# A decoder layer with a mixture of experts: four experts in the last unit, its last product in halves, the last norm's rows spread by the tensor engine

## The chip, the cores and the metric

The kernel runs on one core of one Trainium2 chip. The metric is the device time of one execution in microseconds (us). Before the change the median of three runs is 1271.21 us (1270.5 to 1271.6).

Engines as the profile names them: PE is the tensor engine's matmul side (TensorE), PEld its weight loads, DVE the vector engine, ACT the scalar engine, POOL GpSimd, SP the engine that issues most DMAs. A "q" behind a name (SPq) is that engine's sequencer.

## The reference

One layer of a decoder: a token-mixing part (two kinds of attention, an output projection and a norm) and then a mixture of experts with a last norm. The change touches only the end of the second part:

```python
h = _layer_norm(x) * (1 + sc2[:, None]) + sh2[:, None]
y = (1 + g2[:, None]) * _hier_moe(h, ...)          # 32 experts, two for each of 512 tokens
x = _layer_norm(ALPHA * x + y) * ln2_g[l] + ln2_b[l]

def expert_block(args):                            # in _hier_moe
    xb, e = args
    return (jax.nn.silu(xb @ w1[e]) * (xb @ w3[e])) @ w2[e]
```

The data is float32: 512 tokens of 1024 features, each expert has w1 and w3 of 1024 x 512 and w2 of 512 x 1024, 2 MB each, 6 MB an expert.

## The kernel before

All 32 experts' weights are read, some 200 MB. The experts are sorted by how many tokens they got, and worked in **units** of 128 token slots: one expert with 128 slots, two with 64 or four with 32. After two fixed units (-2 and -1) the list `ORDER` says in which order the eleven others come. A unit number of 2 to 6 is a pair (64 slots each), 7 to 10 a unit of four (32 slots each); before, the list ends with unit 10 (four experts) and unit 6 (two).

**Loads.** `load_unit` (L1249) issues a unit's weights on SP's queue: t counts 0 to 11, four tiles of 512 KB for each of w1, w3 and w2 and each expert, so 24 tiles for a pair and 48 for four. Tiles come from a ring of 36 buffers (`Q`, which other tiles share), in order of allocation. A plain tile is `src[:, j * 1024:(j + 1) * 1024]`, a contiguous 4 KB for each of 128 partitions. With `quarters` (the last unit) a tile of w2 holds 256 of the 1024 output columns for all four row blocks k, which is four pieces of 1 KB for each partition: 512 pieces a tile (L1266). Every 512 KB tile is one DMA.

**Work of a unit.** `up` makes silu(x w1) * (x w3) on PE, ACT and DVE; between the two products (`mid=between`) the previous unit's results are added to the four accumulators `acc[i]` (128 tokens x 1024) by `combine`. `down_lhs` transposes the result (`pat` to `aT`) and the routing weights (`ptw` to `pT`). For four experts each product runs on 32 columns of the array (form 128*32), for two on 64 (128*64).

**The last unit** has its own product with w2, in four quarters q of 256 columns. `quarter_up` makes `py` (8 products), `weighted_halves` (L1493 to L1496) makes `y` (DVE), its rounded copy `yh` (ACT) and the rest `yl` (DVE); `quarter_add` spreads them over the tokens by eight products `pcb` (yh and yl for four token tiles) and adds them to `acc`, with a running sum for the norm (L1665). `squares` (ACT, L1647) makes the sums of squares around a shift `nsh`, which is a mean from quarter 0. Each engine works strictly in the order of the code. With q equal to 3, between `y` and the adds, stands `overflow()`: a loop over leftover blocks with a count read at run time, where all engines meet (L1542); in this data it has no turn.

**The last norm.** `l2g` and `l2b`, its weight and bias, are read by `row_bc` (L1632, L1633): a DMA on POOL's queue that reads one row of 4 KB 128 times, once for each partition, 512 KB each. `bh` and `bl` are row 0 of `l2b`, rounded and rest. Behind the adds come small DVE operations on `l3`, `less_mean` (L1702) for four token tiles, Ln and Exp on ACT for the deviation, and then two token tiles finish on PE and ACT (`pcl`, L1721) and two on DVE (L1726), each half with a store.

## Time and profile before

| | us |
|---|---|
| runs: median (lowest to highest) | 1271.21 (1270.5 to 1271.6) |
| the profiled execution's own time | 1270.36 |
| its span, first to last instruction | 1268.6 |
| last 512 KB tile in 4 KB pieces issued | 1214.74 |
| first and last quarter tile issued | 1216.67 and 1229.66 |
| first and last quarter's `py` begins | 1230.59 and 1244.25 |
| last `yl` (before the loop) begins | 1248.84 |
| last add of the last unit begins | 1252.44 |

The profile is one execution. Its first page gives busy shares in 40 slices of the span, 31.7 us each; the timeline lists instructions by start, with duration, and in brackets how long the engine was idle before and what ended it. A `x16` behind a float32 product counts profiler records, two for a product in the code. The windows view gives each engine's busy time in a stretch, then the granted TensorE clock (1.00 is 2.4 GHz, 0.50 is 1.2 GHz), the busy share of the DMA engines and the bytes they moved.

### The profile page before, as it was taken

The page shows a single profiled execution, that of the slowest core. Times are in us where ns is not written, and L with a number is a line of the kernel's source. Part 1 is how long each engine was busy: PE and PEld are TensorE (multiplying, and loading weights), DVE is VectorE, ACT ScalarE, POOL GpSimd, SP SyncE. Part 2 cuts the span into 40 slices and gives each one's busy share as a digit, 9 for nine tenths or more (in the row PEclk, how much of TensorE's full clock was granted, in tenths as well). Part 3 has the DMA queues.
Part 4 walks back from the last instruction along what each step waited for, and adds up shares of the span by engine and source line. Part 5 has one row for each costly group of instructions (what it writes and reads, how often), then busy time and mean ns, then how long its engine had stood idle before and what let it go on. Part 6 is the DMA issues. An engine that isn't in the chain of part 4 may idle for free. (4 is left out here: it accounts for less than half of the span.)

```text
span 1268.6 us, 18601 instructions
## 1 busy us (share of the span) xinstructions
PE 1182.0 (93%) x6663; PEld 817.7 (64%) x6663; DVE 698.9 (55%) x1624; ACT 426.1 (34%) x907; POOL 117.2 (9%) x175
## 2 busy tenths in 40 slices
PE   5999999999999999999989969999999899999885
PEld 4788898778888888878768963434335235354233
DVE  5564988887565665323586787435135144444045
ACT  4333666664435264554131421201102002021004
POOL 3011111111101011001150140000000000000000
PEclk8999999999999999999998979999999999999998
DMA  9954313324334253335324098999999999999991
GB/s 323 297 148 145 114 58 117 104 88 129 108 113 120 68 167 100 100 120 184 116 84 183 26 356 304 409 408 409 409 409 409 409 409 408 405 406 409 401 329 68
DMA packets 140863, 297.14 MB, mean 234 GB/s; under 512 B 11100, under 2 KB 82980, under 8 KB 140769
## 3 DMA queue, kind: packets, MB, share of 16 engines
q1 hardware_dynamic: 131296, 268.57, 57.6%
q0 software_dynamic: 8704, 25.00, 6.1%
q10 hardware_dynamic: 768, 2.37, 0.5%
q8 instruction: 53, 0.87, 0.3%
q14 instruction: 42, 0.34, 0.1%
HBM read 293.76 MB, written 4.76 MB: 235 GB/s over the span
## 5 line engine op out<-in xcount | busy, mean ns | idle before, releaser
L183 PE MATMUL p<-ew,xe 128*32 128x512 f32 (+1 forms) x960 | 196.7, 597 | 12.5 <-DMA ew<-in_exp_w_dram 12.4
L276 DVE TENSOR_TENSOR wl<-wst,wh 128x1024 fp32r<-128x1024 f32 (+1 forms) x93 | 126.1, 1385 | 74.7 <-ACT wh L275 73.8
L183 PEld LDWEIGHTS p<-ew,xe 128*32 128x32 f32 (+1 forms) x960 | 53.6, 122 | 149.0 <-issue 79.3
L183 PE MATMUL py<-ew,aT 128*32 128x512 f32 (+2 forms) x496 | 101.6, 571 | 9.3 <-DMA ew<-in_exp_w_dram 6.5
L1472 DVE TENSOR_TENSOR s<-s,p 128x512 f32<-128x512 f32 x13 | 8.9, 688 | 173.2 <-PE p L183 157.4
L275 ACT ACTIVATE wh<-wst 128x1024 fp32r<-128x1024 f32 (+1 forms) x94 | 93.0, 1030 | 28.9 <-POOL wst L274 16.6
L183 PEld LDWEIGHTS py<-ew,aT 128*32 128x32 f32 (+1 forms) x496 | 27.3, 122 | 76.3 <-DMA ew<-in_exp_w_dram 35.9
L1521 DVE TENSOR_TENSOR acc<-acc,pcb 128x512 f32<-128x512 f32 x96 | 58.3, 681 | 15.2 <-PE pcb L181 15.2
L1480 ACT ACTIVATE aT<-pat 128x512 f32<-128x512 f32 x13 | 7.8, 597 | 171.9 <-PE pat L187 171.9
L1495 ACT ACTIVATE yh<-y 128x512 fp32r<-128x512 f32 (+1 forms) x28 | 16.8, 599 | 141.9 <-DVE y L1493 131.8
L181 PE MATMUL pgx<-pm,xhh 128*128 128x256 f32 (+1 forms) x224 | 56.3, 293 | 2.1 <-DVE pm L1241 2.1
L1493 DVE SCALAR_TENSOR_TENSOR y<-py,cs,g2b 128x512 f32<-128x512 f32 (+1 forms) x28 | 19.9, 710 | 65.6 <-PE py L183 65.4
L181 PE MATMUL pgx<-pm,xhl 128*128 128x256 f32 (+1 forms) x224 | 54.6, 286 | 0.0
L514 POOL DMA_DIRECT2D adaw<-in_ada_w_dram x64 | 34.6, 542 | 196.6 <-PE ptp L187 44.0
L181 PE MATMUL pcb<-yh,pT 128*128 128x512 f32 (+1 forms) x112 | 44.6, 400 | 6.9 <-DVEq L1542 3.6
L181 PE MATMUL pmg<-hh,wh 128*128 128x512 f32 x128 | 50.4, 394 | 0.0
L181 PE MATMUL psg<-hh,wh 128*128 128x512 f32 x128 | 50.3, 393 | 0.0
L181 PE MATMUL psg<-hl,wh 128*128 128x512 f32 x128 | 49.9, 390 | 0.0
L181 PE MATMUL psg<-hh,wl 128*128 128x512 f32 x128 | 49.9, 390 | 0.0
L181 PE MATMUL pmg<-hh,wl 128*128 128x512 f32 x128 | 49.9, 390 | 0.0
L181 PE MATMUL pmg<-hl,wh 128*128 128x512 f32 x128 | 49.8, 389 | 0.0
L181 PEld LDWEIGHTS pgx<-pm,xhh 128*128 128x128 f32 x224 | 43.8, 196 | 5.6 <-DVE pm L1241 2.5
(520 smaller groups left out, 2872.8 us busy)
## 6 DMA issues: line engine op xcount, KB each, us to landing
ew<-in_exp_w_dram SPq DMA_DIRECT2D x380, 512.0 KB, 10.1
wst<-in_w_in_dram SPq DMA_DIRECT2D x66, 512.0 KB, 4.7
adaw<-in_ada_w_dram POOLq DMA_DIRECT2D x64, 256.0 KB, 3.1
adaw<-in_ada_w_dram SPq DMA_DIRECT2D x16, 512.0 KB, 9.2
wst<-in_w_br_hg_dram SPq DMA_DIRECT2D x8, 512.0 KB, 4.0
wst<-in_w_br_nsa_dram SPq DMA_DIRECT2D x8, 512.0 KB, 4.1
wst<-in_w_out_dram SPq DMA_DIRECT2D x8, 512.0 KB, 4.9
ext_d<-ext_d POOLq DMA_DIRECT2D x1, 2560.0 KB, 17.1
```

Of the source, the lines that this page charges most:

```text
L181: PE.matmul(o, l, r, start=start, stop=stop)
L183: PE.matmul(o, l, r, start=start, stop=stop, tile_position=pos)
L275: A.activation(wh, self.w[j], AF.Copy)
L276: (sub or V).tensor_sub(wl, self.w[j], wh.bitcast(F32))
L514: P_.dma_start(w, ada[:, k, 2048 + j * 512:2560 + j * 512])
L1472: V.tensor_mul(s1, s1, p3)
L1480: A.activation(aT, at_.rearrange("p (f s) -> p f s", f=4), AF.Copy)
L1493: V.scalar_tensor_tensor(y, py, cs_, g2b[c0 // 512][:, c0 % 512:c0 % 512 + n], op0=OP.mult, op1=OP.mult)
L1495: A.activation(yh, y, AF.Copy)
L1521: V.tensor_add(acc[i][:, s_], acc[i][:, s_], pc_)
```

## The change

`ORDER` swaps its last two units, so the pair 6 comes before the unit of four 10, and the last unit loads 48 tiles where it loaded 24. Its w2 is loaded in halves: a tile holds 512 columns for two row blocks, two pieces of 2 KB for each partition, 256 pieces a tile. The tiles come in the order first half (8 tiles: two row-block pairs times four experts), second half (8 tiles).

The last product runs in two pieces of 512 columns, `half_up` and `half_add`, where there were four of 256. The first half's sums give `nsh`, and its squares come before the second half; the loop stands before the second half's adds. `l2g` and `l2b` are loaded as single rows (`l2r`, 4 KB on one partition each). While the second half's weights come in, ACT and DVE split both rows into a rounded part and a rest (`l2h`, `l2l`), PE multiplies them by a row of ones (eight products into four `pl2` tiles), and ACT copies these into `l2g` and `l2b`. The final steps are as before, with one small addition less.

```diff
-ORDER = [7, 0, 8, 1, 9, 2, 3, 4, 5, 10, 6]
+ORDER = [7, 0, 8, 1, 9, 2, 3, 4, 5, 6, 10]
...
-                if quarters and t >= 8:
-                    nc.sync.dma_start(w.rearrange("p (k n) -> p k n", k=4),
-                                      src.rearrange("p (k n) -> p k n", k=4)[:, :, j * 256:(j + 1) * 256])
+                if halves and t >= 8:
+                    kk, c0 = j % 2 * 2, j // 2 * 512
+                    nc.sync.dma_start(w.rearrange("p (k n) -> p k n", k=2),
+                                      src.rearrange("p (k n) -> p k n", k=4)[:, kk:kk + 2, c0:c0 + 512])
...
-    l2g = row_bc("l2g", a["ln2_g"])
-    l2b = row_bc("l2b", a["ln2_b"])
+    l2r = [Q(n_)[0:1, :] for n_ in ("l2gr", "l2br")]
+    for t, name in zip(l2r, ("ln2_g", "ln2_b")):
+        P_.dma_start(t, a[name])
...
+    def half_up(h):
+        py = PS("py")
         m = 128 // len(w_now["exp_w2"])
         for k in range(4):
             for x, w in enumerate(w_now["exp_w2"]):
-                mm(py[m * x:m * x + m, :], aT[:, k, m * x:m * x + m], w[q][:, k * 256:(k + 1) * 256], k == 0, k == 3,
-                   pos=(0, m * x) if m < 128 else None)
+                mm(py[m * x:m * x + m, :], aT[:, k, m * x:m * x + m], w[2 * h + k // 2][:, k % 2 * 512:k % 2 * 512 + 512],
+                   k == 0, k == 3, pos=(0, m * x) if m < 128 else None)
...
-    for q in range(4):
-        py = quarter_up(q)
-        y = quarter_y(q, py)
-        if q == 3:
-            overflow()
-            A.preload_act_table_set("natural_log_exp_and_others")
-            V.tensor_reduce(l3[:, :, 4:5], sums[:, :, 0:3], axis=AX.X, op=OP.add)
-        if q == 2:
-            for i in range(NT):
-                squares(i, 0)
-        if q == 1:
-            oner, bh, bl = (Q(n_, F32R)[0:1, :] for n_ in ("oner", "l2h", "l2l"))
-            A.activation(oner[:, 0:128], ones[0:1, :], AF.Copy)
-            A.activation(bh, l2b[0:1, :], AF.Copy)
-            V.tensor_sub(bl, l2b[0:1, :], bh.bitcast(F32))
-        for i in range(NT):
-            quarter_add(q, y, i)
-            if q > 1:
-                squares(i, q - 1)
-        if q == 0:
-            V.tensor_scalar(nsh, sums[:, :, 0], -1.0 / 256, None, op0=OP.mult)
+    py = half_up(0)
+    y = weighted_halves(py, cs_, 0, 512)
+    oner = Q("oner", F32R)[0:1, 0:128]
+    A.activation(oner, ones[0:1, :], AF.Copy)
+    l2h, l2l = ([Q(n_, F32R)[0:1, :] for n_ in ns] for ns in (("l2gh", "l2bh"), ("l2gl", "l2bl")))
+    for t, h_, l_ in zip(l2r, l2h, l2l):
+        A.activation(h_, t, AF.Copy)
+        V.tensor_sub(l_, t, h_.bitcast(F32))
+    for i in range(NT):
+        half_add(0, y, i)
+    V.tensor_scalar(nsh, sums[:, :, 0], -1.0 / 512, None, op0=OP.mult)
+    l2g, l2b = Q("l2g"), Q("l2b")
+    for t, h_, l_ in zip((l2g, l2b), l2h, l2l):
+        for s_ in halves_:
+            ps = PS("pl2")
+            for j, x in enumerate((h_, l_)):
+                mm(ps, oner, x[:, s_], j == 0, j == 1)
+            A.activation(t[:, s_], ps, AF.Copy)
+    for i in range(NT):
+        squares(i, 0)
+    py = half_up(1)
+    y = weighted_halves(py, cs_, 512, 512)
+    overflow()
+    A.preload_act_table_set("natural_log_exp_and_others")
+    for i in range(NT):
+        half_add(1, y, i)
+        squares(i, 1)
...
-    V.tensor_add(l3[:, :, 3], sqs[:, :, 0], sqs[:, :, 1])
```

Where the instructions go, at two places. First ScalarE (ACT), from the rounded copy `yh` of quarter 1 (with the change: of the first half) to the last `yh` before the loop. Here `sq` are the squares, `acc_6756` and its likes the four token tiles, and the column counts at the end tell quarters (256) from halves (512). Before:

```order
L1495 ACTIVATE yh_10857<-y_10855 128x256
L1684 ACTIVATE oner_10861<-ones_94 1x128
L1685 ACTIVATE l2h_10862<-l2b_10791 1x1024
L1495 ACTIVATE yh_10894<-y_10892 128x256
L1647 ACTIVATE sq_10812,sqs_10811<-acc_6756,nsh_10813 128x512
...
L1647 ACTIVATE sq_10812,sqs_10811<-acc_7244,nsh_10813 128x512
L1647 ACTIVATE sq_10812,sqs_10811<-acc_6756,nsh_10813 128x256
...
L1647 ACTIVATE sq_10812,sqs_10811<-acc_7244,nsh_10813 128x256
L1495 ACTIVATE yh_10933<-y_10931 128x256
```

The same stretch with the change:

```order
L1496 ACTIVATE yh_10817<-y_10815 128x512
L1673 ACTIVATE oner_10821<-ones_94 1x128
L1676 ACTIVATE l2gh_10823<-l2gr_10773 1x1024
L1676 ACTIVATE l2bh_10824<-l2br_10774 1x1024
L1687 ACTIVATE l2g_10848<-pl2_10850 128x512
...
L1687 ACTIVATE l2b_10849<-pl2_10862 128x512
L1648 ACTIVATE sq_10796,sqs_10795<-acc_6756,nsh_10797 128x512
...
L1648 ACTIVATE sq_10796,sqs_10795<-acc_7244,nsh_10797 128x512
L1496 ACTIVATE yh_10889<-y_10887 128x512
```

The eight squares that stood ahead of the last `yh` are four, and ahead of them stand the split of a second row and four copies out of `pl2`.

Second PE, from the product before the last one to the loop, where `py` is the product with w2 (`ew` the weights), `pcb` the spread over the tokens. Before:

```order
L183 MATMUL py<-ew,aT 64x256 x8
L181 MATMUL pcb<-yh,pT 128x256
L181 MATMUL pcb<-yl,pT 128x256
...
L183 MATMUL py<-ew,aT 64x256 x8
L1542 COMPARE_AND_BRANCH
```

With the change (the `pl_` tiles are the `pl2` of the code):

```order
L183 MATMUL py<-ew,aT 32x512 x16
L181 MATMUL pcb<-yh,pT 128x512
L181 MATMUL pcb<-yl,pT 128x512
...
L181 MATMUL pl_10850<-l2gh,oner 128x512
L181 MATMUL pl_10850<-l2gl,oner 128x512
...
L181 MATMUL pl_10862<-l2bh,oner 128x512
L181 MATMUL pl_10862<-l2bl,oner 128x512
L183 MATMUL py<-ew,aT 32x512 x16
L1543 COMPARE_AND_BRANCH
```

Eight products `pl2` now stand between the first half's `pcb` and the second half's `py`, and each `py` is sixteen products of 512 columns in place of eight of 256.

## Rows read from the trace of the kernel before

**Rows 1.** Page, part 2: busy tenths of the DMA engines in 40 slices.

```profile
DMA  9954313324334253335324098999999999999991
```

**Rows 2.** Windows: busy us (instructions), PE PEld DVE ACT POOL; clock; DMA share, GB/s.

```profile
30.00:40.00 10.00, 10.00 (x72) 7.71 (x70) 2.75 (x6) 1.52 (x2) 0.00 (x0) 1.00 1.09 348
1200.00:1205.00 5.00, 4.54 (x16) 0.82 (x16) 0.75 (x1) 0.54 (x1) 0.00 (x0) 1.00 1.02 405
1240.00:1245.00 5.00, 3.69 (x32) 2.33 (x28) 3.98 (x18) 2.64 (x7) 0.00 (x0) 1.00 0.00 0
1245.00:1250.00 5.00, 1.42 (x13) 0.75 (x10) 1.02 (x5) 3.64 (x13) 0.00 (x0) 0.94 0.02 5
1250.00:1256.00 6.00, 5.56 (x16) 4.00 (x16) 4.41 (x18) 4.28 (x12) 0.00 (x0) 0.50 0.00 1
```

**Rows 3.** SP's issues of L1269, 1191 to 1206 us and 1190 to 1215 us.

```profile
L1269 SPq DMA_DIRECT2D ew<-in_exp_w_dram x13: 333/333/337, 1191.1 to 1206.4; - x13
...
DMA to landing us min/median/max: 9.6/10.1/12.7
...
L1269 SPq DMA_DIRECT2D ew<-in_exp_w_dram x19: 332/333/337, 1189.9 to 1214.7; - x19
```

**Rows 4.** Timeline of POOL, 1206 us: the first of two row loads.

```profile
1206.60 0.59 POOL L973 DMA_DIRECT2D l2g<-in_ln_g_dram  x1 [448.68 <-DVE y L1493]
```

**Rows 5.** SP's issues of L1266, quarter tiles: ns min/median/max, times.

```profile
L1266 SPq DMA_DIRECT2D ew<-in_exp_w_dram x8: 543/1180/3129, 1216.7 to 1229.7; - x8
```

**Rows 6.** Timeline of the last unit (start, us, engine, line): first and last quarter.

```profile
1230.59 1.95 PE L183 MATMUL py<-ew,aT 128*64 128x256 f32 x16 [0.25 <-ACT aT L1480]
...
1244.25 1.95 PE L183 MATMUL py<-ew,aT 128*64 128x256 f32 x16
...
1248.40 0.40 ACT L1495 ACTIVATE yh<-y 128x256 fp32r<-128x256 f32 x1
1248.84 0.43 DVE L1496 TENSOR_TENSOR yl<-y,yh 128x256 fp32r<-128x256 f32 x1 [2.10 <-ACTq L1542]
```

**Rows 7.** Timeline behind the loop: adds, row products, the norm's last products.

```profile
1249.78 0.58 PE L181 MATMUL pcb<-yh,pT 128*128 128x256 f32 x1 [3.58 <-DVEq L1542]
...
1251.34 0.17 DVE L1677 TENSOR_REDUCE l<-sums 128x4 f32<-128x12 f32 x1 [2.07 <-PE pcb L181]
...
1252.38 0.62 PE L181 MATMUL pcl<-l2l,oner 1*128 1x512 f32 x1
...
1252.44 0.42 DVE L1665 CUSTOM_DVE_ANT_0 acc<-acc,pcb 128x256 f32<-128x256 f32 x1
...
1252.80 0.62 PE L181 MATMUL pcl<-l2h,oner 1*128 1x512 f32 x1
...
1256.37 5.30 PE L181 MATMUL pcl<-acc,dg 128*128 128x512 f32 x8 [0.81 <-ACT dg L1715]
```

**Rows 8.** Timeline of earlier units: y, yh, yl, eight adds, py of 512 columns.

```profile
937.83 0.75 DVE L1493 SCALAR_TENSOR_TENSOR y<-py,cs,g2b 128x512 f32<-128x512 f32 x1 [13.31 <-PE py L183]
...
938.62 0.63 ACT L1495 ACTIVATE yh<-y 128x512 fp32r<-128x512 f32 x1 [14.82 <-DVE y L1493]
...
939.28 0.69 DVE L1496 TENSOR_TENSOR yl<-y,yh 128x512 fp32r<-128x512 f32 x1 [0.69 <-ACT yh L1495]
...
953.29 4.86 DVE L1521 TENSOR_TENSOR acc<-acc,pcb 128x512 f32<-128x512 f32 x8
...
1202.53 1.90 PE L183 MATMUL py<-ew,aT 128*32 128x512 f32 x10 [0.24 <-DMA ew<-in_exp_w_dram]
```

**Rows 9.** Timeline of the last unit: the split of a row, the squares.

```profile
1238.15 1.04 ACT L1685 ACTIVATE l2h<-l2b 1x1024 fp32r<-1x1024 f32 x1
...
1239.23 1.21 DVE L1686 TENSOR_TENSOR l2l<-l2b,l2h 1x1024 fp32r<-1x1024 f32 x1 [0.72 <-ACT l2h L1685]
...
1242.62 0.71 ACT L1647 ACTIVATE sq<-acc,nsh 128x512 f32<-128x512 f32 x1
...
1246.00 0.51 ACT L1647 ACTIVATE sq<-acc,nsh 128x256 f32<-128x256 f32 x1
```

More of the change, by code (lines that the diff above doesn't have):

```diff
@@ L1247, in expert_rows, with load_unit @@
         return a[name][0][ds(e, 1)].rearrange("e (p k) n -> p (e k n)", p=128)
-    def load_unit(es, lo=0, hi=12, res=None, quarters=False):
+    def load_unit(es, lo=0, hi=12, res=None, halves=False):
         res = res or {n: [[] for _ in es] for n in ("exp_w1", "exp_w3", "exp_w2")}
@@ L1561, in overflow @@
             for i in range(NT):
-                V.tensor_reduce(sums[:, i, 0:3], acc[i][:, 0:768].rearrange("p (q n) -> p q n", q=3), axis=AX.X, op=OP.add)
+                V.tensor_reduce(sums[:, i, 0:1], acc[i][:, 0:512], axis=AX.X, op=OP.add)
                 squares(i, 0)
-                squares(i, 1)
         S = s_ring
@@ L1615, in hybrid_kernel @@
             es = tuple(ev(4 * v_ - 16 + x) for x in range(4))
-        w_now, quarters = ws, n + 2 == len(units)
-        ws = load_unit(es, quarters=quarters)
+        w_now, halves = ws, n + 2 == len(units)
+        ws = load_unit(es, halves=halves)
         if n > 1:
@@ L1630, in hybrid_kernel, with squares @@
     w_now = ws
-    l2g = row_bc("l2g", a["ln2_g"])
-    l2b = row_bc("l2b", a["ln2_b"])
+    l2r = [Q(n_)[0:1, :] for n_ in ("l2gr", "l2br")]
+    for t, name in zip(l2r, ("ln2_g", "ln2_b")):
+        P_.dma_start(t, a[name])
     aT, pT, cs_ = down_lhs(act, pw)
     l3 = cp.tile([128, NT, 6], F32, name="l3")
-    sums = cp.tile([128, NT, 4], F32, name="sums")
-    sqs = cp.tile([128, NT, 3], F32, name="sqs")
+    sums = cp.tile([128, NT, 2], F32, name="sums")
+    sqs = cp.tile([128, NT, 2], F32, name="sqs")
     sq = S("sq")
     nsh = cp.tile([128, NT], F32, name="nsh")
-    def squares(i, j):
-        c0, n = ((0, 512), (512, 256), (768, 256))[j]
-        A.activation(sq[:, 0:n], acc[i][:, c0:c0 + n], AF.Square, bias=nsh[:, i:i + 1], accum_out=sqs[:, i, j:j + 1])
-    def quarter_up(q):
-        py = PS("py")[:, 0:256]
+    halves_ = [slice(0, 512), slice(512, 1024)]
+    def squares(i, h):
+        A.activation(sq, acc[i][:, halves_[h]], AF.Square, bias=nsh[:, i:i + 1], accum_out=sqs[:, i, h:h + 1])
+    def half_up(h):
+        py = PS("py")
         m = 128 // len(w_now["exp_w2"])
@@ L1654, in quarter_up @@
             for x, w in enumerate(w_now["exp_w2"]):
-                mm(py[m * x:m * x + m, :], aT[:, k, m * x:m * x + m], w[q][:, k * 256:(k + 1) * 256], k == 0, k == 3,
-                   pos=(0, m * x) if m < 128 else None)
-        return py
-    def quarter_add(q, y, i):
-        pc_ = PS("pcb")[:, 0:256]
+                mm(py[m * x:m * x + m, :], aT[:, k, m * x:m * x + m], w[2 * h + k // 2][:, k % 2 * 512:k % 2 * 512 + 512],
+                   k == 0, k == 3, pos=(0, m * x) if m < 128 else None)
@@ L1662, in quarter_add, with half_add @@
+        return py
+    def half_add(h, y, i):
+        pc_ = PS("pcb")
         for j, t in enumerate(y):
             mm(pc_, pT[:, i * 128:(i + 1) * 128], t, j == 0, j == 1)
-        z = acc[i][:, q * 256:(q + 1) * 256]
+        z = acc[i][:, halves_[h]]
         V.tensor_tensor_reduce(out=z, in0=z, in1=pc_, scale=1.0, scalar=0.0, op0=OP.add, op1=OP.add,
-                               accum_out=sums[:, i, q:q + 1])
-    def quarter_y(q, py):
-        return weighted_halves(py, cs_, q * 256, 256)
@@ L1694, in hybrid_kernel @@
-    V.tensor_add(l3[:, :, 0], sums[:, :, 3], l3[:, :, 4])
+                               accum_out=sums[:, i, h:h + 1])
+    py = half_up(0)
[8 more added lines that the diff above has]
+        half_add(0, y, i)
@@ L1695, in hybrid_kernel @@
+    for i in range(NT):
+        half_add(1, y, i)
+        squares(i, 1)
+    V.tensor_add(l3[:, :, 0], sums[:, :, 0], sums[:, :, 1])
     V.scalar_tensor_tensor(l3[:, :, 2], l3[:, :, 0], 1.0 / D, nsh, op0=OP.mult, op1=OP.add)
     V.tensor_mul(l3[:, :, 2], l3[:, :, 2], l3[:, :, 2])
-    V.tensor_add(l3[:, :, 3], sqs[:, :, 0], sqs[:, :, 1])
-    V.scalar_tensor_tensor(l3[:, :, 5], l3[:, :, 3], 1.0 / D, l3[:, :, 2], op0=OP.mult, op1=OP.subtract)
+    V.scalar_tensor_tensor(l3[:, :, 5], sqs[:, :, 0], 1.0 / D, l3[:, :, 2], op0=OP.mult, op1=OP.subtract)
@@ L1703, in hybrid_kernel @@
     less_mean(0)
-    V.scalar_tensor_tensor(l3[:, :, 1], sqs[:, :, 2], 1.0 / D, l3[:, :, 5], op0=OP.mult, op1=OP.add)
+    V.scalar_tensor_tensor(l3[:, :, 1], sqs[:, :, 1], 1.0 / D, l3[:, :, 5], op0=OP.mult, op1=OP.add)
     A.activation(l3[:, :, 2], l3[:, :, 1], AF.Ln, bias=eps[:, 0:1])
@@ L1708, in hybrid_kernel @@
     dg = S("dg")[:, 0:256].rearrange("p (i t) -> p i t", i=2)
-    halves_ = [slice(0, 512), slice(512, 1024)]
     pcl = {(i, h): PS("pcl") for i in range(2) for h in range(2)}
     for (i, h), ps in pcl.items():
-        for j, b_ in enumerate((bh, bl)):
+        for j, b_ in enumerate((l2h[1], l2l[1])):
             mm(ps, oner[:, 0:128], b_[:, halves_[h]], j == 0, False)
```

## The prediction

> **What bounds the kernel now.** I read the page's slices first. From slice 24 on (about 760 us) the DMA engines stand at nine tenths or more almost to the end, and only the last slice is empty [rows 1]: in this stretch the experts' weights set the pace. The windows say how fast: 405 GB/s between 1200 and 1205 us, nothing at all from 1240 us [rows 2]. So the kernel ends in two parts, a stream that ends before 1240 us and some 30 us of work behind it, and the question is what in that work waits for weights.
>
> SP's issues give the stream's pace: 13 tiles of 512 KB from 1191.1 to 1206.4 us, which is 12 steps of 1.275 us, each landing 10.1 us after its issue [rows 3]. The nineteen issues up to 1214.7 us take 24.8 us where 18 such steps are 23.0 [rows 3]; between them POOL issued the two spread row loads [rows 4].
>
> Then the last unit. Its first quarter starts at 1230.59 us, its fourth at 1244.25 [rows 6]: 4.55 us a quarter, with 1.95 us of PE in it. The last quarter tile was issued at 1229.7 us [rows 5], and the fourth quarter starts over 4 us after the last bytes have moved [rows 2]. The quarters wait for each other, not for weights: py, y, yh, yl, spread, next py, each on another engine. The last `yh` moreover starts at 1248.40 us without an idle time of ACT ahead of it [rows 6], so it stood in line behind the eight squares. `yl` ends at 1248.84 + 0.43 = 1249.27 us; call this point **E**. From E to the end of the span it is 19.3 us: the loop, the adds (the last ends at 1252.44 + 0.42 = 1252.86 us [rows 7]) and the norm with its stores.
>
> **The change, step by step.** With a unit of four last, 16 tiles of w2 come behind the last tile of w3. The first half's product, its spread and the rows then have time while the second half loads, so E should follow the end of the stream. Call the landing of the last tile T.
>
> *The stream's end.* The 1206.4 us issue was ahead of the spread row loads; it lands at 1206.4 + 10.1 = 1216.5 us. Five of the 19 issues in rows 3 come after it (19 less 13 and the one at 1189.9), and the eight quarter tiles [rows 5], so 13 tiles follow. The change swaps two units, not the number of tiles. The two spread loads, 1 MB, are gone from the 16 engines, two steps or 2.55 us; two rows of 4 KB are nothing. The tiles of w2 are now in 2 KB pieces, which this trace doesn't show in a full stream. Bounds: 4 KB pieces at 1.275 us a tile [rows 3]; 1 KB pieces (the 256-column loads of the start) at 348 GB/s between 30 and 40 us [rows 2], 524,288 B / 348 = 1.507 us. A tile has 128, 256 or 512 pieces, so I go by a price for each piece: 1.275 + 0.232 x 128/384 = 1.352 us. The two tiles ahead of the 13 are halves too, 0.15 us more. T = 1216.5 + 13 x 1.352 + 0.15 = **1234.2** us (bounds 1233.1 and 1236.6).
>
> The Trainium skill (DMA: Bandwidth & Descriptors, Specifications) gives 512 B as the smallest transfer at line rate; by that rule halves would cost as much as whole rows, and quarters too. The trace speaks against it for 1 KB.
>
> *From T to E.* The order of the products is row block, then expert, so behind the last tile five products are left. In earlier units of four the same five (ten records) took 1.90 us from the landing [rows 8]. Then y, yh, yl of 512 columns: from 937.83 to 939.28 + 0.69, 2.14 us [rows 8], and 0.05 us to start. E = 1234.2 + 1.90 + 0.05 + 2.14 = **1238.3** us, against 1249.27: **11.0 us earlier**.
>
> *What has to be hidden before.* The first half's last tile lands at T - 8 x 1.352 = 1223.4 us; aT is ready long before, since w3 ended eight tiles earlier still. py ends at 1225.3, the first yh at 1226.8 (0.84 to its start, 0.63 [rows 8]). On ACT follow two row splits of 1.04, on DVE two rests of 1.21 [rows 9]: DVE is through at about 1230.5, because the adds stand behind the rests in DVE's order. Four adds of 512 at 4.86/8 = 0.61 us [rows 8] and nsh: 1233.2. The spread's eight products on PE and four copies on ACT (0.6 each, as yh) fit before that. Then four squares, 1246.00 - 1242.62 = 3.38 us with their reads [rows 9]: ACT is free at 1236.6, and the second yh wants it at 1234.2 + 1.90 + 0.05 + 0.79 = 1236.9. Cover 0.3 us: it costs nothing, but each microsecond more on this side chain costs nearly one. On PE the eleven products of the second half whose tiles have landed stand behind the spread; they begin at about 1231.5 and end about when T comes.
>
> *Behind E.* The loop stays. PE's first product starts 0.51 us after E (1249.78), DVE's first operation 2.07 us after it (1251.34) [rows 7]. Before, the adds then ended 3.59 us after E. Now they have 512 columns. The clock has fallen to half here [rows 2], where row products of 512 columns start 0.42 us apart (1252.38, 1252.80 [rows 7]); four pairs end at 0.51 + 7 x 0.425 + 0.62 = 4.1 us, and the last add, some 0.15 + 0.69 us, at 4.95. That is **1.36 us later** than before. The smaller DVE chain (one small addition) I leave at nothing; from the last add on I take the old 15.74 us.
>
> *Sum.* 1268.6 - 11.0 + 1.36 = **1259.0** us of span. The profiled execution has 1.76 us beside its span (1270.36), and the median of the runs lies 0.85 us above that execution: 1259.0 + 1.76 + 0.85 = **1261.6** us.
>
> **The rivals.**
>
> *The clock stays up.* PE idles 3.58 us ahead of the first spread product behind the loop [rows 7], and the granted clock goes from 0.94 to 0.50 in those windows [rows 2]: that is the fall from 2.4 to 1.2 GHz. With the change PE ends its last product at 1236.1 and starts again at 1238.8, 2.7 us. If that isn't idle enough, the pairs come 0.43 us apart and DVE sets the adds: 2.07 + 4 x 0.61 + 0.1 = 4.6 (-0.35), and the norm's last products, 5.30 us at mostly half clock [rows 7], lose up to 1.9, of which DVE's two token tiles, that end nearly as late, let through about 1.2. Time 1261.6 - 1.5 = **1260.1**. For it: the gap is shorter. Against: PE has little to do in the gap's neighbourhood either. The Trainium skill (TensorE: Matmul & The Clock Gate, part 1) says that throttled is the default state and activity releases it, which leaves both open.
>
> *Halves at full rate.* If a piece of 2 KB costs no more than its bytes, the 16 tiles come at the 1.275 us of whole rows [rows 3]: T is 1233.1, the time 1261.6 - 1.1 = **1260.5**. For it: whole rows show no price for their own pieces. Against: 1 KB pieces have one [rows 2]. This is also what the Trainium skill's rule above would make of it.
>
> *The side chain comes late.* If the row splits, adds and squares take 2.3 us longer than my sum (a late row, a PSUM buffer not free, squares that wait), the second yh waits 2 us for ACT: **1263.6**. For it: a margin of 0.3 us. Against: all durations are from rows.
>
> *The stream's end doesn't move as said*: the share of the two spread loads isn't won, because the ring of 36 buffers holds up a last unit of 48 tiles for as long. T is then 2.55 us later, the time **1264.2**. Against: units of four ran at the full pace with the same ring, as the slices before the end show [rows 1].
>
> *SP's issues stall, slower than before.* Quarter tiles cost SP 0.54 to 3.13 us to issue, 1.86 us apart in the mean (1216.7 to 1229.7 in seven steps [rows 5]) against 0.33 for a whole tile [rows 3]. With the change this falls on 16 tiles of which the last binds. At 1.86 us a tile T is 13 x 0.51 = 6.6 us later, **1268.2**. At 2.28 us a tile the change is slower by 0.2%; at 2.7, the upper half of what rows 5 show, the time is 1261.6 + 13 x 1.37 = **1279.4**. For it: halves still have twice the pieces of whole rows. Against: at the start 1 KB pieces kept 348 GB/s [rows 2].
>
> **How the numbers follow.** Forecast 1261.6: 0.45. Clock stays: 0.2. Halves at full rate: 0.1. Side chain late: 0.12. Stream's end unmoved: 0.05. Stalls: 0.08, of which 0.03 end on the slower side and 0.01 within. The runs can tell about 0.2% (2.5 us) from no change. Faster: 0.96; same 0.01; slower 0.03. The range goes from 1258.5 (4 KB rate and the clock up, with the side chain then binding) to 1266.0 (past the upper bound of T, 1261.6 + 2.4, and the unmoved stream); it leaves out the stalls and the tails of the rest, under 2 in 10.
>
> **What would show it.** Right: the last `ew` tile lands near 1234 us, `py` starts its last five products only then, the last `yl` ends about 4.1 us later, ACT has a short idle time or none ahead of the last `yh`, and the last add ends 4.6 to 5 us behind `yl`. SP's half tiles should issue about 1.35 us apart, with issues under 1 us. Wrong: issues of 2 us or more; a `yh` that follows the squares without a gap and late; a stream whose end stays at 1238 us; or an end part that isn't as long as before.

## The result, and the profile after

The changed kernel takes 1264.83 us (median of seven runs, 1261.01 to 1266.71) where the kernel before, run beside it, takes 1270.5 (1269.99 to 1271.6): a ratio of 0.995, 95% interval 0.9937 to 0.9963. The forecast was 1261.6 with a range of 1258.5 to 1266.0. The profiled execution took 1264.83 us with a span of 1263.0, 4.0 more than the 1259.0 of the sum.

First the page's slices of the kernel after, to be held against [rows 1]: the granted clock and the DMA engines' busy tenths.

```profile
PEclk9999999999999999999998989999999999999996
DMA  9954314234334243335335097999999999999991
```

The stream still fills the end up to the last slice. SP's issues of the half tiles, which answer to [rows 3] and [rows 5] (times in ns: min/median/max):

```profile
L1267 SPq DMA_DIRECT2D ew<-in_exp_w_dram x16: 372/413/1245, 1202.3 to 1222.8; - x16
...
DMA to landing us min/median/max: 10.3/11.0/11.5
```

Sixteen issues from 1202.26 to 1222.83 us are 15 steps of 1.371 us. The last tile lands 10.5 us after its issue, so T is 1233.3 us. Now the timeline, which answers to [rows 6], [rows 7] and [rows 9]:

```profile
1222.75 1.90 PE L183 MATMUL py<-ew,aT 128*32 128x512 f32 x10 [1.03 <-DMA ew<-in_exp_w_dram]
...
1226.16 0.49 PE L181 MATMUL pcb<-yh,pT 128*128 128x512 f32 x1 [1.50 <-ACT yh L1496]
...
1229.37 0.79 PE L181 MATMUL pl<-l2gh,oner 1*128 1x512 f32 x1
...
1232.53 0.62 PE L181 MATMUL pl<-l2bl,oner 1*128 1x512 f32 x1
...
1233.08 6.11 PE L183 MATMUL py<-ew,aT 128*32 128x512 f32 x32
...
1236.84 0.18 ACT L1648 ACTIVATION_READ_ACCUMULATOR sq<-acc,nsh 128x1 f32 x1
...
1240.05 0.63 ACT L1496 ACTIVATE yh<-y 128x512 fp32r<-128x512 f32 x1 [3.02 <-DVE y L1494]
1240.71 0.69 DVE L1497 TENSOR_TENSOR yl<-y,yh 128x512 fp32r<-128x512 f32 x1 [0.70 <-ACTq L1543]
...
1241.97 0.80 PE L181 MATMUL pcb<-yh,pT 128*128 128x512 f32 x1 [2.78 <-DVEq L1543]
...
1245.55 0.68 DVE L1666 CUSTOM_DVE_ANT_0 acc<-acc,pcb 128x512 f32<-128x512 f32 x1
...
1249.67 6.42 PE L181 MATMUL pcl<-acc,dg 128*128 128x512 f32 x8 [2.19 <-ACT dg L1717]
```

E is 1240.71 + 0.69 = 1241.40 us (1241.41 unrounded). The second half's sixteen products (x32) run in one piece, without any wait for a DMA, from 1233.08 to 1239.19 us. So the last tile, at 1233.3, was not what they waited for: PE came late to them, and was slow. ACT, for which the prediction had 0.3 us of cover, waited 3.02 us for their `y`. The windows of the same kernel, one microsecond each, with the columns of [rows 2], show why:

```profile
1225.00:1226.00 1.00, 0.00 (x0) 0.00 (x0) 0.44 (x1) 0.52 (x1) 0.00 (x0) 1.00 1.06 391
1226.00:1227.00 1.00, 0.61 (x2) 0.30 (x3) 0.69 (x1) 1.00 (x3) 0.00 (x0) 1.00 0.95 348
1227.00:1228.00 1.00, 1.00 (x5) 0.78 (x6) 0.71 (x1) 1.00 (x2) 0.00 (x0) 0.93 0.38 145
1228.00:1229.00 1.00, 1.00 (x4) 0.63 (x2) 1.00 (x2) 0.20 (x1) 0.00 (x0) 0.50 0.11 43
...
1232.00:1233.00 1.00, 1.00 (x3) 0.33 (x2) 0.23 (x3) 0.68 (x2) 0.00 (x0) 0.50 0.05 18
```

The clock falls to 1.2 GHz between 1227 and 1228 us and stays there until 1238.1. Ahead of it PE had run the first half's product with waits of about a third of a microsecond to one for tiles, and had idled 1.5 us for `y` and `yh`. The last two columns show something else: the bytes all but stop at 1227.5 us, and 18 to 43 GB/s trickle until the last tile is in, over 5 us later. The trace's semaphore records tell more of it. A tile has landed when its semaphore has been raised sixteen times; for the last tile fifteen of these fall between 1227.00 and 1229.00 us, and the sixteenth comes alone at 1233.28. In the eleven profiled executions with halves the last tile's sixteenth comes 3.9 to 4.8 us behind its fifteenth. That fits one of the core's 16 DMA engines that ends late (385 / 16 = 24 GB/s, about the trickle); which engine it is, and why, is not shown.

The change's 19 runs beside all the experiments (1261.01 to 1267.64, median 1264.48) fall in two groups with nothing between: eight up to 1262.79 and eleven from 1264.42. Three of the 19 executions are profiled; what is known of the cause is told with e12 and behind the experiments.

### The profile page after: what moved, and what is told of

Same layout as the page of the kernel before. It is cut to its first block, busy times and chain, and to the rows that moved or that the text cites. A ratio compares the mean times of both kernels' runs of the same rounds, so it can differ in the third digit from the quotient of the medians.

```text
span 1263.0 us, 18494 instructions
## 1 busy us (share of the span) xinstructions
PE 1178.2 (93%) x6623; PEld 815.2 (65%) x6623; DVE 696.5 (55%) x1603; ACT 428.0 (34%) x902; POOL 115.5 (9%) x175
## 5 line engine op out<-in xcount | busy, mean ns | idle before, releaser
L276 DVE TENSOR_TENSOR wl<-wst,wh 128x1024 fp32r<-128x1024 f32 (+1 forms) x93 | 119.6, 1315 | 74.8 <-ACT wh L275 74.1
L183 PE MATMUL py<-ew,aT 128*32 128x512 f32 (+1 forms) x464 | 98.1, 621 | 8.8 <-DMA ew<-in_exp_w_dram 6.0
L1496 ACT ACTIVATE yh<-y 128x512 fp32r<-128x512 f32 x26 | 16.4, 631 | 133.8 <-DVE y L1494 122.2
L1494 DVE SCALAR_TENSOR_TENSOR y<-py,cs,g2b 128x512 f32<-128x512 f32 x26 | 19.4, 748 | 66.3 <-PE py L183 66.1
L181 PE MATMUL pcb<-yh,pT 128*128 128x512 f32 x104 | 43.8, 422 | 4.3 <-DVEq L1543 2.8
```

Source lines behind the costliest of these rows:

```text
L181: PE.matmul(o, l, r, start=start, stop=stop)
L183: PE.matmul(o, l, r, start=start, stop=stop, tile_position=pos)
L276: (sub or V).tensor_sub(wl, self.w[j], wh.bitcast(F32))
L1494: V.scalar_tensor_tensor(y, py, cs_, g2b[c0 // 512][:, c0 % 512:c0 % 512 + n], op0=OP.mult, op1=OP.mult)
L1496: A.activation(yh, y, AF.Copy)
```

## The experiments

Theory: E comes late because PE's clock is at half ahead of and during the second half's product; with the clock up, that product waits for T and E is T + 4.1 as forecast. Rivals: the slow last landing sets E whatever the clock; the new order gives nothing and the gain is that of halves and rows; the order gives it all. One number tells the first two apart: E behind the last tile's issue. The measured landing of 10.5 us and the 4.1 us of the prediction make 14.6; the profile above has 18.58. "Unread products" are products of 512 columns on the whole array whose result nothing reads.

All profiled executions in one table (us). S is the issue of the first tile behind the pause that ends the routing stage, where the even stream starts: 766.60 in before.

| kernel | ratio to before (95%) | S | last issue, S + | E, S + | E behind last issue | last add, E + | from there to the end |
|---|---|---|---|---|---|---|---|
| before | 1 | 766.60 | 463.1 | 482.7 | 19.60 | 3.60 | 15.72 |
| after | 0.9950 (0.9937, 0.9963) | 765.35 | 457.5 | 476.1 | 18.58 | 4.83 | 16.73 |
| e7, after again | 0.9948 (0.9933, 0.9965) | 768.84 | 456.9 | 475.5 | 18.58 | 4.78 | 16.75 |
| e12, after again | 0.9941 (0.9926, 0.9956) | 767.96 | 456.6 | 471.2 | 14.54 | 4.63 | 16.03 |
| e2, order only | 0.9956 (0.9941, 0.9970) | 767.63 | 463.7 | 475.8 | 12.12 | 3.93 | 16.62 |
| e3, pair last | 0.9977 (0.9965, 0.9988) | 767.70 | 456.8 | 476.9 | 20.06 | 4.63 | 16.50 |
| e4, spread loads | 0.9951 (0.9936, 0.9965) | 767.12 | 459.4 | 473.9 | 14.55 | 4.63 | 15.84 |
| e1, unread products | 0.9946 (0.9929, 0.9962) | 765.34 | 456.5 | 471.0 | 14.55 | 5.73 | 14.04 |
| e8, e1 again | one run | 767.29 | 457.1 | 472.6 | 15.49 | 6.01 | 17.60 |
| e5, bias late | 0.9940 (0.9926, 0.9955) | 767.65 | 457.2 | 471.7 | 14.56 | 4.63 | 17.95 |
| e6, unread between | 0.9981 (0.9968, 0.9993) | 767.65 | 456.5 | 477.5 | 21.04 | 5.42 | 15.50 |
| e9, late and 11 unread | 0.9936 (0.9922, 0.9950) | 767.67 | 456.6 | 471.1 | 14.56 | 5.44 | 15.60 |
| e11, late and 6 unread | 0.9924 (0.9911, 0.9938) | 767.38 | 457.0 | 471.6 | 14.56 | 4.63 | 16.64 |
| e10, before and 12 unread | 1.0005 (0.9996, 1.0014) | 767.13 | 462.4 | 482.0 | 19.60 | 4.05 | 16.88 |

**e1: unread products in three places.**

```diff
     py = half_up(0)
+    warm(6)                  # 6 unread products
...
     py = half_up(1)
+    warm(10)
...
     # behind the norm's bias products pcl
+    warm(8)
```

> Edit: products whose result nobody reads are put into PE's idle times of the changed kernel: 6 behind the first half's product, 10 behind the second half's, 8 behind the bias products of the norm. In the changed kernel's trace the granted clock is at half from 1227.8 to 1238.1 us and again around the adds and the norm's last products; PE had waited for y and yh ahead of each fall. Theory A (the fallen clock makes PE the last to arrive: the second half's product takes 6.1 us and ends 5.9 us behind the landing of the last tile, 1222.8 + 10.5 = 1233.3): with the clock up the product ends 1.9 us behind that landing, so about 4 us earlier, the adds about 0.3 and the last products about 1.5 earlier: a span of about 1257.5, time near 1259, and the runs closer together. Theory B (the stream's end and the length of the chain set the time, the clock is a side effect): span 1262 to 1264, no change within 0.1%.

E came 14.55 us behind the last issue, not 18.58, at a clock that stayed up until 1252.2 us; the profiled execution took 1257.89 us, the shortest of all runs. The norm's products show what the clock is worth there:

```profile
1245.51 3.70 PE L181 MATMUL pcl<-acc,dg 128*128 128x512 f32 x8 [0.52 <-ACT dg L1725]
```

3.70 us where the kernel after took 6.42. The last tile took the same 10.4 us to land, so the rival that the landing sets E at 18.6 falls. But the median is 1263.73 and three of six runs lie above 1264.4: the unread products did not hold the clock each time, and the ten in front of the loop cost the adds 0.9 us (E + 5.73).

**e2: the new order alone**, in the kernel before.

```diff
-ORDER = [7, 0, 8, 1, 9, 2, 3, 4, 5, 10, 6]
+ORDER = [7, 0, 8, 1, 9, 2, 3, 4, 5, 6, 10]
```

> Edit: the kernel before with only the order of the last two units swapped; four quarters, quarter tiles in 1 KB pieces and the two spread row loads as before. Theory A (the order makes the stream's end the point from which the tail counts): the stream has 16 quarter tiles and 1 MB of row loads, so its last tile lands at 1239 (1.5 us a tile) to 1244 us (1.86 us a tile, as the eight quarter tiles before); E follows 3.5 us later, and the end 19.3 us after E: span 1262 to 1266.5, some 2 to 6 us faster than before. Theory C (the order is worth nothing by itself, the halves and the row loads make the gain): span 1268 to 1270.

The order alone gives a ratio of 0.9956, nearly the whole gain of the median. SP's issues of its sixteen quarter tiles, and the timeline up to the last `yl`:

```profile
L1266 SPq DMA_DIRECT2D ew<-in_exp_w_dram x16: 543/1183/5711, 1204.1 to 1231.3; - x16
```

```profile
1239.81 1.92 PE L183 MATMUL py<-ew,aT 128*32 128x256 f32 x26 [0.75 <-SPq L1542]
...
1242.07 0.51 ACT L1647 ACTIVATE sq<-acc,nsh 128x256 f32<-128x256 f32 x1
...
1242.58 0.40 ACT L1495 ACTIVATE yh<-y 128x256 fp32r<-128x256 f32 x1
1243.01 0.43 DVE L1496 TENSOR_TENSOR yl<-y,yh 128x256 fp32r<-128x256 f32 x1 [0.77 <-ACTq L1542]
```

With four quarters behind the stream, the order by itself brings E 6.9 us nearer to S. But its last issue is 6.2 us later than in the kernel after. The sixteen tiles of 1 KB pieces come 1.81 us apart (27.2 us in 15 steps), where halves take 1.37. Not all of this is the price of the pieces, because the two spread row loads, 1 MB, run in the same stretch. POOL issues the first here, and only 1 KB pieces of weights move in the windows from 1220 us on (columns as in [rows 2]):

```profile
1209.21 0.59 POOL L973 DMA_DIRECT2D l2g<-in_ln_g_dram  x1 [451.01 <-DMA ew<-in_exp_w_dram]
```

```profile
1220.00:1225.00 5.00, 3.86 (x28) 1.38 (x28) 0.25 (x1) 0.00 (x0) 0.00 (x0) 0.68 0.94 309
1225.00:1230.00 5.00, 3.42 (x40) 2.52 (x40) 2.77 (x12) 0.57 (x2) 0.00 (x0) 0.98 1.05 332
1230.00:1235.00 5.00, 3.72 (x34) 2.04 (x38) 3.00 (x10) 1.41 (x3) 0.00 (x0) 1.00 1.05 343
```

309 to 343 GB/s are 1.53 to 1.70 us a tile. `yh`, again without an idle time ahead of it, stands behind eight squares. One thing more sets this kernel apart: its times are 2.45 to 2.70 us above their spans in all six runs, those of every other kernel 1.73 to 1.91. By the span (median 1263.5, the 19 runs of the changed kernel 1262.6) the order alone is nearer still to the whole change. Where the 0.7 us come from is not shown.

**e3: everything but the order.** The changed kernel with the old `ORDER`, so halves and rows with a pair last (the e2 line the other way round).

> Edit: the changed kernel with the old order, the pair last, so with halves and single rows only. Theory A: the pair's work isn't bound by loads; w3 lands 2.5 us earlier than before (no spread row loads), and two serial halves with the split of the rows between them take about as long as four quarters less the squares: E near 1244 and a span near 1264, 1 us slower than the changed kernel and 4 to 5 us faster than before; so most of the gain is the halves and the row loads, and the order adds little. Theory D (the order is the whole gain): span 1267 or more.

The ratio is 0.9977, about half of the gain or less. The span of 1265.7 us is neither that of theory A (1264) nor that of theory D (1267 or more). Its timeline:

```profile
1238.44 3.65 PE L183 MATMUL py<-ew,aT 128*64 128x512 f32 x16
...
1242.14 0.75 DVE L1494 SCALAR_TENSOR_TENSOR y<-py,cs,g2b 128x512 f32<-128x512 f32 x1 [2.17 <-PE py L183]
...
1242.54 0.72 ACT L1648 ACTIVATE sq<-acc,nsh 128x512 f32<-128x512 f32 x1
...
1243.26 0.61 ACT L1496 ACTIVATE yh<-y 128x512 fp32r<-128x512 f32 x1
```

The whole product of the second half (3.65 us, no wait for a tile) comes behind the spread, and `yh` behind four squares: E is 20.1 us behind the last issue. With a pair, w3 ends only eight tiles before the end, so the first half's chain is not over when the last tile lands. The order alone (0.44%) and halves with rows alone (0.23%) each pay, and together they come to more than the whole change (0.50 to 0.59%), though the intervals leave room for a plain sum. That both shorten the same stretch is likely, not shown.

**e4: the two spread loads back**, no rows spread by PE, in the changed kernel.

```diff
+    l2g = row_bc("l2g", a["ln2_g"])
+    l2b = row_bc("l2b", a["ln2_b"])
-    l2r = ...                # the rows' loads, the split of the weight's row
-    ...                      # eight products pl2, four copies
```

> Edit: the changed kernel with the two rows loaded 128 times each by POOL again, and without the split of the weight row, the eight products that spread the rows and the four copies. Theory A (PE, not the stream, arrives last in the changed kernel): the stream ends 2.5 us later, at about 1235.9, but PE has 3.7 us less ahead of the second half's product; E is at 1240 to 1241.5 against 1241.4, span 1261.5 to 1263: the same as the changed kernel. Theory B (the stream's end sets the time): 2.5 us slower than the changed kernel, span near 1265.5.

The last tile is issued at S + 459.4, 1.9 to 2.9 us later than in the changed kernel's other forms: that is the price of the two loads (2.55 in the prediction). But PE's clock stayed up through the second half's product here, and E is again 14.55 us behind the last issue. E and the span (1241.06 and 1261.5 us) are where theory A had them, but not for its reason: E follows the landing by 4.1 us, so here the stream sets it. The median, 1264.72 us, is that of the changed kernel. Rows instead of spread loads won nothing in the median. That the eight products of one row and 512 columns ahead of the second half take back what the stream gives, whenever the clock is low there, fits this but is not shown by the medians.

**e5: the bias row's spread moved** behind the norm's bias products, where PE waits.

```diff
-    for t, h_, l_ in zip((l2g, l2b), l2h, l2l):   # 8 products, 4 copies
+    # 4 products and 2 copies for l2g here
...
+    pl2b = spread(1)         # 4 products for l2b, behind the products pcl
```

> Edit: in the changed kernel the bias row's four spread products and its two copies are moved from ahead of the second half's product to behind the bias products of the norm, where PE waited 2.2 us and ACT 1.9 us in the changed kernel's trace. Theory A (PE arrives last): the second half's product starts four row products earlier, 0.9 us at the full clock and 1.7 at half, and ACT is free 1.2 us earlier: span 1261 to 1262, 0.1% faster than the changed kernel. Theory B (the stream's end sets the time): no change.

E behind the last issue is 14.56 us, 4.0 less than in the kernel after, and no run is above 1264.23 us. The median is 1263.76 us, beside 1264.73 of e7 in the same set, with intervals that overlap. The clock then falls behind E (1240.7 to 1254.4 us at 1.2 GHz), the norm's products take 6.59 us, and the end comes 17.95 us after the last add: 1.2 of the 4.0 are given back there.

**e6: e5 with unread products between the products of the first half**, and with six behind that half, ten behind the second and four behind the late bias products.

```diff
             mm(py[m * x:m * x + m, :], ...)
+            if fill and k % 2 == 0 and k + x < 5:
+                warm(fill)   # 3 unread products behind each of 7 products
```

> Edit: the kernel e5_bias_late with unread products in PE's waits: three behind each of the first products of the first half that wait for a tile, six behind that half, ten behind the second half, four behind the late bias products. The profiled execution of e1_warm kept the full clock to the loop and had a span of 1256.1, but its other executions took up to 8 us more. Theory A (the clock's falls, at places that differ from run to run, are the spread and the missing 3 us): a span of 1255.5 to 1257.5 with the clock up from 1215 us to the loop, and a median under 1261. Rival E (the spread between executions comes from ahead of the last unit, where the stream starts later or earlier by up to 2 us, and not from the tail): the median stays within 1 us of e1_warm's, 1263 to 1264.

A miss, and for a plain reason:

```profile
1227.31 1.05 PE L183 MATMUL py<-ew,aT 128*32 128x512 f32 x2
1228.29 0.96 PE L181 MATMUL dum<-pT 128*128 128x512 f32 x3
1229.18 1.04 PE L183 MATMUL py<-ew,aT 128*32 128x512 f32 x2
1230.15 0.96 PE L181 MATMUL dum<-pT 128*128 128x512 f32 x3
```

PE was to fill its waits for tiles. But a product on 32 columns of the array and three on all of it take 1.87 us one after the other, more than the 1.37 us in which a tile comes. PE fell behind the stream, the first half ended 6 us late, and E came 21 us behind the last issue. The clock did stay up until 1246.8 us, which was worth nothing by then. Eleven of the twelve runs took 1267.71 us or more; one took 1262.74, which this reason does not cover.

**e7: the changed kernel again.**

> The changed kernel again, unedited, for another profiled execution and for times beside the other kernels of this batch. Theory A: if the clock falls at another place of the tail, or not ahead of the second half's product, E moves by up to 4 us against 1241.4 while the landing of the last tile stays 10.5 to 11 us behind its issue; the median is near 1265. Rival E: E stays the same number of us behind the last issue, and the times differ by where the stream starts.

The rival holds for this execution. E is again 18.58 us behind the last issue, with the clock at half from 1230.8 to 1241.0 us; the 2.9 us by which E comes later than in the first profile lie in the start of the stream (S 768.84 against 765.35).

**e8: e1 again.**

> The kernel e1_warm again, one look. Theory A: the time follows from whether the clock stays up in the tail; with it up the span is 1256 to 1258, and a span over 1260 shows a half-clock stretch between 1215 and 1252 us. Rival E: a span over 1260 shows the full clock in the tail and a last issue later than 1221.8 us by the difference.

The clock fell 0.8 us into the second half's product (1233.1 us), after PE had worked without a gap through the eight row products. The product, and the windows around it (columns as in [rows 2]):

```profile
1232.30 5.34 PE L183 MATMUL py<-ew,aT 128*32 128x512 f32 x32
```

```profile
1230.00:1235.00 5.00, 5.00 (x30) 2.25 (x32) 3.77 (x11) 3.19 (x7) 0.00 (x0) 0.81 0.08 27
1235.00:1240.00 5.00, 5.00 (x30) 2.31 (x22) 1.45 (x3) 2.76 (x7) 0.00 (x0) 0.85 0.00 2
```

E is 15.49 us behind the last issue. So unread products with all eight row products still in front of the second half don't keep the clock for certain.

**e9: e5 with six unread products behind the first half and five behind the second.**

```diff
     py = half_up(0)
+    warm(6)
...
     py = half_up(1)
+    warm(5)
```

> The changed kernel with the bias row's spread moved behind the norm's bias products (as in e5_bias_late), and eleven unread full-array products: six behind the first half's last product, five behind the second half's; all that the reference wants is still computed. If the clock over the second half's product is what makes E (the end of the last yl) come 18.58 us behind the last half tile's issue and not 14.55, E is here 14.4 to 14.8 us behind it, the last add ends at E+4.6 to 4.9, the end comes 14.0 to 15.8 us after that and the median is 1260.0 to 1262.0 us. Rival: the clock falls all the same, only later, within the adds and the norm, E+17 us or more to the end after the last add, and the median stays at 1263.0 to 1264.5 us, as in e1_warm and e5_bias_late.

E behind the last issue is 14.56 us as expected, and the runs keep together (1261.63 to 1263.67); the median, 1262.28 us, lies just above the expected stretch. The adds missed theirs: with the five unread products PE's first spread product starts 1.32 us behind E, not 0.51 as in e11 without them, and the last add comes at E + 5.44.

**e10: twelve unread products behind the last quarter's product of the kernel before.**

```diff
     for q in range(4):
         py = quarter_up(q)
+        if q == 3:
+            ...              # 12 unread products
```

> The kernel before with twelve unread full-array products behind the last quarter's product and nothing else; all that the reference wants is still computed. It prices the clock behind E in the old order: if the fall there can be held off by busy columns, the last add stays at E+3.6 or up to 0.6 us less, the end comes 1.0 to 2.0 us sooner after it than the 15.74 us of before, and the ratio is 0.998 to 0.999. Rival: the unread products only make the engine late to its loop of adds (E+4.5 or more) or the clock falls in another place of the tail, and the ratio is 0.9995 to 1.001.

The rival holds: the clock falls elsewhere in the tail. PE was busy for 3.06 us in the old gap, and the clock fell 2.7 us later instead (1252.1 us, not 1249.4); the last add moved from E + 3.60 to E + 4.05 and the ratio is 1.0005:

```profile
1245.97 3.06 PE L181 MATMUL dum<-pT 128*128 128x512 f32 x12
...
1251.17 0.39 PE L181 MATMUL pcb<-yh,pT 128*128 128x256 f32 x1 [2.15 <-issue]
```

**e11: e9 without the last five unread products.**

```diff
     py = half_up(1)
-    warm(5)
```

> The changed kernel with the bias row's spread behind the norm's bias products and six unread full-array products behind the first half's last product, none behind the second half's; all that the reference wants is still computed. If eleven unread products in e9_late_warm5 made the tensor engine late to the loop (last add E+5.44) and otherwise paid nothing behind E, here the last add is back at E+4.6 to 4.7, E stays 14.4 to 14.8 us behind the last half tile's issue, and the end comes 16 to 18 us after the last add because the clock falls there; the median is 1261.5 to 1263.5 us, within 1 us of e9_late_warm5's. Rival: without columns behind the second half the whole tail runs at half clock and the median is 1264 us or more, no better than the changed kernel.

The last add is back at E + 4.63, E is 14.56 us behind the last issue and the median is 1261.74 us, the lowest of all. Its second half's product in the timeline, and the windows behind E:

```profile
1231.39 3.24 PE L183 MATMUL py<-ew,aT 128*32 128x512 f32 x22
...
1234.86 1.90 PE L183 MATMUL py<-ew,aT 128*32 128x512 f32 x10 [0.24 <-SPq L1543]
```

```profile
1240.00:1245.00 5.00, 4.53 (x19) 3.06 (x17) 3.68 (x14) 3.94 (x9) 0.00 (x0) 1.00 0.00 2
1245.00:1250.00 5.00, 2.98 (x4) 1.44 (x5) 5.00 (x6) 2.93 (x9) 0.00 (x0) 0.54 0.00 0
```

Eleven products (x22) run as soon as the spread is over, PE waits, and the last five (x10) take 1.90 us from the landing, in the form that the prediction drew.

**e12: the changed kernel beside e11.**

> The changed kernel itself beside e11_late_warm_first on one chip. If the half clock over the second half's product costs it time that six unread products and the late bias save, its median lies 1.5 to 4 us above that of e11_late_warm_first, at 1263.5 to 1265.5 us, with E 16 to 18.6 us behind the last half tile's issue. Rival: both medians lie within 1 us of each other, since the clock that is held up in one place falls in another.

The medians are 1262.49 and 1261.74 us, 0.75 apart, with intervals that overlap: the rival holds, this set does not tell the two kernels apart. The profiled execution, 1261.66 us, is worth more than the comparison, because in it the clock held. SP's issues, and the timeline:

```profile
L1267 SPq DMA_DIRECT2D ew<-in_exp_w_dram x16: 373/384/1180, 1204.0 to 1224.6; - x16
```

```profile
1224.52 1.90 PE L183 MATMUL py<-ew,aT 128*32 128x512 f32 x10 [0.97 <-DMA ew<-in_exp_w_dram]
...
1227.93 0.50 PE L181 MATMUL pcb<-yh,pT 128*128 128x512 f32 x1 [1.51 <-ACT yh L1496]
...
1230.48 0.50 PE L181 MATMUL pl<-l2gh,oner 1*128 1x512 f32 x1
...
1232.20 0.38 PE L181 MATMUL pl<-l2bl,oner 1*128 1x512 f32 x1
1232.51 4.44 PE L183 MATMUL py<-ew,aT 128*32 128x512 f32 x32
...
1237.78 0.63 ACT L1496 ACTIVATE yh<-y 128x512 fp32r<-128x512 f32 x1 [0.35 <-DVE y L1494]
1238.44 0.69 DVE L1497 TENSOR_TENSOR yl<-y,yh 128x512 fp32r<-128x512 f32 x1 [0.70 <-ACTq L1543]
1239.69 0.50 PE L181 MATMUL pcb<-yh,pT 128*128 128x512 f32 x1 [2.74 <-DVEq L1543]
```

It is the same program, with the same waits of PE ahead of the spread (0.97 and 1.51 us; 1.03 and 1.50 in the first profile), but the row products are 0.23 us apart instead of 0.43, and the product takes 4.44 us instead of 6.11. One window of each, first this execution, then the first profile:

```profile
1230.00:1235.00 5.00, 5.00 (x33) 2.16 (x31) 4.01 (x11) 2.96 (x7) 0.00 (x0) 1.00 0.08 27
```

```profile
1230.00:1235.00 5.00, 5.00 (x20) 2.52 (x22) 2.23 (x9) 3.57 (x7) 0.00 (x0) 0.50 0.06 20
```

## Why the prediction was right, and where it was wrong

The sign and the range held, and so did the mechanism in the executions in which the clock holds; the forecast was 3.2 us below the median. That the range holds the median all the same is in part luck: its upper end was made for a slower stream (T past its bound, or the row loads' share not won), not for PE's clock. By the prediction's terms:

*T, the landing of the last tile: right.* Forecast 1234.2, measured 1233.3. The stream of the profiled execution started 1.25 us sooner than that of before; put right for this, the forecast is 1232.95 and the miss 0.35 us. In e12, where it started 1.36 us later, it is 1235.56 against 1235.01. A half tile costs 1.371 us where the interpolation gave 1.352, and no issue stalled SP: 0.37 to 1.25 us. (Two slips change nothing: three halves, not two, lie ahead of the sum's thirteen tiles, 0.08 us; and the dearest price of the stalls is 13 x 1.35, not 1.37, so 1279.1.) The rivals "halves at full rate" and "stalls" fall. Late in the stream too, pieces of 1 KB moved at 309 to 343 GB/s (the windows of e2) and pieces of 2 KB at 382 (524,288 B in 1.371 us), beside the 405 of [rows 2] for 4 KB. That stands against the rule of the Trainium skill (DMA: Bandwidth & Descriptors, Specifications), which gives 512 B as the smallest transfer at line rate.

*From T to E: the step that failed.* Forecast 4.1 us, measured 8.1. It is the sentence by which PE's eleven products "begin at about 1231.5 and end about when T comes", and behind it the assumption that the clock falls only behind E. The clock fell at the first half's spread, behind idle times for tiles and for `yh` that the change itself puts there; since e12 has the same ones, they are not shown to be the cause of the fall. The eight row products then took 3.7 us instead of 2.0, and the second half's product 6.1 instead of 3.65, so that PE, not the stream, set E. With the clock up the step is right to 0.1 us: E - T is 4.12 in e12, and E behind the last issue 14.54 to 14.56 us in e1, e4, e5, e9, e11 and e12, against 18.58 twice with the clock at half. That is 4.0 us, shown in one and the same program: 2.3 us because the second half's product starts 0.2 us ahead of T and not 2.5, and 1.7 us because it takes 6.11 us and not 4.44. Of its 19 runs the profiled 1264.83 and 1267.64 are in the upper group, 1261.66 in the lower; that the clock parts the other sixteen as well fits their mean granted clock (0.978 to 0.983 in the lower group, 0.975 to 0.978 in the upper) but is not shown. The place of the stream moves the time as well: S is 765.35 and 768.84 in the upper two, 767.96 in the lower one.

*The side chain: right, and the cover too.* Forecast 0.3 us of cover for ACT ahead of the last `yh`; e12 has 0.35. In the first profile it is 3.02, because `y` was late. How thin it is e3 shows, where `yh` waits for the squares.

*Behind E: right.* Forecast E + 4.95, measured 4.83 with half clock for most of the adds and 4.63 with the clock up at their start, which is the 4.6 of the rival "the clock stays up".

*From the last add to the end: mis-sized by 1.0 us.* 16.73 instead of 15.74: the norm's products ran at half clock for 5.5 of their 6.42 us, where those of [rows 7], 5.30 us long, had it for 3.2. The time from the last add to these products (3.4 and 3.5 us) and from their end to the span's end (6.9) is nearly the same in both. Across all runs this part takes 14.04 to 17.95 us: least in e1, whose norm products run at full clock, most in e5, where the clock is low for nearly the whole of it.

*The sum.* -0.9 (T) + 4.0 (E) - 0.1 (adds) + 1.0 (end) = 4.0, the whole of 1263.0 - 1259.0. The median misses by 3.2 and not 4.0, because the forecast added 0.85 us for the place of the profiled execution among the runs, and this one is the median itself. For e12 it is +0.8 + 0.0 - 0.3 + 0.3 = 0.8, and its span is 1259.8. So the forecast describes the executions in which the clock holds, and put 0.45 on them without having named the other case: a clock that falls earlier was not among the rivals. The one on the clock looked only at a gain.

*What the parts are worth.* The order: 0.9956 alone. The halves under the new order: 4.3 us at the last issue (e2 against e4, S + 463.7 and 459.4), but 1.35 us in the median (1266.07 against 1264.72 in the same set), of which 0.7 lies outside the span. The profiles say where most of it goes: the last half tile takes 10.4 us from its issue to its landing and the last quarter tile 8.45, and from there to E it is 4.1 us instead of 3.7, so E comes only 1.9 us sooner (S + 475.8 and 473.9). In the quarter tile the sixteenth increment comes 1.6 us behind the fifteenth, in the half tile 4.8. Rows: nothing in the median. e11 wins most, with a ratio of 0.9924; head to head it isn't told apart from the changed kernel. Without a run above 1264.23, though, stand the 16 runs of e5, e9 and e11, all with the bias row late, against 11 of 19 of the changed kernel. (In e6 it is late too, but there PE falls behind the stream.)

*Left open.* Why the same program's clock falls at its 1227.9 us in one execution and at 1241.0 in another. The instructions ahead of that are the same and PE's waits nearly so. In e8 the clock fell at 1233.1 us, with PE busy for the whole of 1230 to 1235 us. The Trainium skill (TensorE: Matmul & The Clock Gate, part 1) says that throttled is the default and activity releases it, which names the danger; it does not tell these executions apart.

## What to carry to other kernels

When a change makes an engine wait for a stream near the end, price that engine's work at both clock levels ahead of the new bound as well as behind it: here 4 us, as much as two thirds of the gain. Products that aren't urgent (the spread of a row) are worth a try behind the critical one: with the bias row there, E came 4.0 us sooner in e5, 1.2 of which the tail lost again, and the gain in the median was 1.0 us, not clear of the spread of the runs. Filling waits with extra products of another array form made them longer (e6). And compare profiles from the start of the stream, not from zero: its place alone moved by 3.5 us between executions of one program.

## What the runs showed of the hardware

- The last 512 KB tile lands over 5 us behind the end of the bulk: 385 to 391 GB/s up to 1226 us, 18 to 43 from 1228 to 1233 us. Fifteen of its sixteen semaphore increments are there by 1229.0 us, the last at 1233.3. The landing time (10.5 us) is the largest part of the 14.55 us from the last issue to E. A last quarter tile (1 KB pieces) took 8.4 us to land in before, e2 and e10.
- Near the end of the stream DMA pieces of 4 and 2 KB cost 1.275 and 1.371 us a 512 KB tile; with 1 KB pieces it was 1.53 to 1.70 us (309 to 343 GB/s in e2). At 1 KB, SP's issues themselves took up to 5.7 us.
- Unread products did not hold the clock for certain: none of the six profiled executions with them is free of half clock in the tail. In e10 the fall came at 1252.1 us instead of 1249.4. Whether they moved it is not shown, since the fall moves by more than 10 us between executions of the changed kernel without any.
- Products on 32 columns and on the whole array hardly overlap: 1.05 and 0.96 us gave a step of 1.87 us (e6).
